# Sample state operations behind the third value tile, masks a head at a time on two engines, and one gate-up weight piece in a place of its own

## Chip, core and metric

The kernel runs on one core of a Trainium2 chip. The metric is device time in microseconds (us) of one execution, as a median over executions. An execution under the hardware profiler gives the trace; its own time is a little longer than the span of the trace, which leaves out what lies before the first and behind the last instruction.

The engines: TensorE (PE in the profile; PEld is its weight load), VectorE (DVE), ScalarE (ACT), GpSimd (POOL) and SyncE (SP), which issues most of the transfers between DRAM and SBUF. Each engine works through its own instructions in order and waits where a result or a buffer isn't ready.

## Reference

One inference step of a one-layer decoder: 8 sample tokens, each with a state of its own, and a prompt of 512 tokens, together 520 columns, with a width of 1024.

```python
z = x @ w_in
qk, mv, mi, mf, mo, aq, ak, av, gm, ga = jnp.split(z, split_points(), axis=-1)
qk, conv_state = causal_dwconv(qk, conv_buf, conv_w, conv_b)
mq, mk = jnp.split(qk, 2, axis=-1)
h, C, n, m = mlstm_chunkwise(mq..., mk..., mv..., mi + b_igate, mf + b_fgate, C0, n0, m0)
...
y_a, k_win, v_win = window_attention(aq..., ak..., av..., k_buf, v_buf, attn_sinks, start)
mixed = jax.nn.sigmoid(gm) * y_m + jax.nn.sigmoid(ga) * y_a
x = layer_norm(ALPHA * x + mixed @ w_out, ln1_g, ln1_b)
g, u = jnp.split(x @ w_gate_up, 2, axis=-1)
ffn = (jax.nn.silu(g) * u) @ w_down
ple = jax.nn.sigmoid(x @ w_ple_gate) * (p @ w_ple)
x = layer_norm(ALPHA * x + ffn + ple, ln2_g, ln2_b)
```

Inside `mlstm_chunkwise` the weights of a chunk are `exp(dmat - m_t)` with a causal mask on `dmat`, and the new state is, per head, `decay_prev * n + sum(w_state * k)` and the same with `k` times `v` for `C`. For a sample token that is one step: `n_new = d * n + w * k`, `C_new = d * C + w * k v`. All is float32.

## The kernel before

**Number format.** A float32 product is made of three products in a faster format: each operand is split into a high part (`split`, line 218, a copy on ScalarE) and the rest (line 219, a subtraction on VectorE or GpSimd), and `mm3`/`mm3ab` (lines 228, 245) add hi·hi, hi·lo and lo·hi. So a weight must be split before TensorE can use it.

**Weights.** They come in blocks of 1 MB through SP's queue into `raw`, a ring of two buffers. `prep_next` splits the next piece of 128 columns into rings `whi` and `wlo` of three buffers each, or into a place of its own where `dest[piece]` names one. `get(piece, ahead)` returns a piece and has later ones prepared.

**Tiles of the input projection.** Tile `t` is 128 columns of `z`: 48 matmuls (8 k-steps, three products, two halves of 264 and 256 columns). Tiles 0 to 7 are q and k of the mLSTM (`ev_qk`), 8 to 15 its values (`ev_mv`, `f` 0 to 7), then the attention's and the gates'. Each tile is evicted behind its matmuls. `ev_mv` copies a value tile from PSUM into `stg`, a ring of two buffers (ACT, L984), transposes it back on TensorE (L987, and L992 for the sample tokens), and copies that to `vaug` (VectorE, L988) and to `tmp` (L996), from where a head's 256 sample values go to a DRAM scratch `vsd` (L998).

**Side work.** `sd.run(t)` issues, behind each tile, steps of lists that were added with a first and a last tile:
- `gate_rows`: the gates' prefix sums and stabilisers; the rows go to a DRAM scratch `bcd` (L912) and come back on all partitions as `wdb` (L913, the sample tokens).
- `conv_out`: the last rows before the convolution, transposed, copied (L973) into a buffer of the ring `stg` and sent out.
- `smlstm_prep`: `n` of the sample tokens is loaded and transposed (L1099), `kws` (L1102, L1103) and `nst` (L1104, L1105) are made from it and `wdb`, `qn` (L1106), and `nst` is transposed back (L1109) and sent out (L1113).
- `ml0`, once a head: two rows of `bcd` on all partitions (L1036, L1037), and the causal mask `cmask` (`amaskA` in the profile) added to the first, chunk by chunk, on GpSimd (L1040).
- `ml1` to `ml3`, once a head and chunk of 128 tokens: the prompt's mLSTM; L1054 is the exponential of a masked chunk.
- `sm0`, `sm1`, `sm2`, once a head and 4 sample tokens: `sm0` loads the state (L1120) and brings `v` from `vsd` to all partitions (L1121, into a `big` buffer); `sm1` scales it by `kws` (ACT, L1141, four times) and updates the state.

Most buffers are rings: `g2` has five of 128x512, `stg` two of 128x520, `tmp` four, PSUM has four banks in `pss` and four in `psm`. A ring's next user waits for the last reader of the buffer, transfers included.

**Order.** In most of the program a scheduler that models the engines' times sets each engine's order from the code and its dependencies; `after(f, ..., f_=[ins])` orders what `f` issues behind `ins` on the engine of `ins`. So a changed step can move others around it. The first gate-up block is a stretch in written order: five weight pieces (`k_gu` to `k_gu + 4`; 3 and 4 in places of their own) are used for the first half of the columns while the first LayerNorm runs, then the second half is computed for four of them. Behind it come pieces from `k_gu + 5` on, each prepared as `get` asks for it, and `tsum`/`tsplit` (L1492, L1496, and L219 on `tf`), which prepare sums of activations for the Strassen products of line 1601.

Of the kernel before, what the change touches and what calls it, by code (L numbers as in the profile page):

```python
# [12 lines left out]
ALU = mybir.AluOpType  # L13
# [4 lines left out]
P = 128  # L18
D = 1024
KD = D // P  # L20
NS = 8
NP = 512
NT = NS + NP
# [6 lines left out]
NCH = NP // P  # L30
# [20 lines left out]
def tile_hybrid_step(  # L51
# [9 lines left out]
    V, S, G, T = nc.vector, nc.scalar, nc.gpsimd, nc.tensor  # L61
# [24 lines left out]
    def ring(tag, n, bufs, p=P):  # L86
        return wp.tile([p, n], F32, tag=tag, name=nm(tag), bufs=bufs)
# [3 lines left out]
    def slab(i):  # L91
        return up.tile([P, U], F32, tag=f"T{i}", name=nm(f"T{i}_"))
# [4 lines left out]
    def v3(t):  # L97
        t3 = t[:, : KD * NT].rearrange("p (j c) -> p j c", j=KD)
        return [t3[:, j, :] for j in range(KD)]
# [89 lines left out]
    def prep_next():  # L189
        i = state["prep"]  # L190
        if i >= len(pieces):
            return
        state["prep"] += 1
        bi_, a, k0, kc, pcol, last = pieces[i]
        if i in dest:
            hi, lo = dest[i]
        else:
            hi = ring("whi", 1024, 3)[:, : kc * pcol].rearrange("p (k n) -> p k n", k=kc)
            lo = ring("wlo", 1024, 3)[:, : kc * pcol].rearrange("p (k n) -> p k n", k=kc)
        split(hi, lo, raws[bi_][:, k0 : k0 + kc, a : a + pcol], G if i in pool_lo else V)  # L200
        ready[i] = (hi, lo)
        if last:
            raws.pop(bi_)
            load_next()

    dest = {}
# [66 lines left out]
    cmask = amaskA[:, :P]  # L273
# [174 lines left out]
    def after(f, *a, f_=None):  # L448
        with ExitStack() as st:
            for ins in f_ or fence:  # L450
                st.enter_context(tc.issue_after(ins))
            f(*a)
# [220 lines left out]
    def g2():  # L673
        return t1([P, 512], "g2", 5)
# [292 lines left out]
    def conv_out():  # L967
        for g in range(2):
            ps = pss()
            for i in range(4):  # L970
                T.transpose(ps[:11, i * P : (i + 1) * P], cvo[:, 4 * g + i, :], ident)
            ost = ring("stg", NT, 2)
            V.tensor_copy(ost[:11, :512], ps[:11, :])  # L973
            nc.sync.dma_start(o_convs[0, :, 2, g * 512 : (g + 1) * 512], ost[:NS, :512])
            nc.sync.dma_start(o_convp[0, 0, :, g * 512 : (g + 1) * 512], ost[NS:11, :512])
            yield
# [4 lines left out]
    def ev_mv(f, pss2):  # L981
        vT = ring("stg", NT, 2)
        for psx, (c0, n) in zip(pss2, HALVES):
            S.activation(vT[:, c0 : c0 + n], psx[:, :n], AF.Copy)  # L984
        ps = pss()
        for c in range(NCH):
            T.transpose(ps[:, c * P : (c + 1) * P], vT[:, NS + c * P : NS + (c + 1) * P], ident)  # L987
        V.tensor_copy(  # L988
            vaug()[:, :, f // 2, (f % 2) * P : (f % 2 + 1) * P], ps.rearrange("p (c d) -> p c d", c=NCH)
        )  # L990
        ps = pss()
        T.transpose(ps[:NS, :P], vT[:, :NS], ident)  # L992
        h = f // 2
        if f % 2 == 0:
            vsx[h] = ring("tmp", 264, 4)
        V.tensor_copy(vsx[h][:NS, (f % 2) * P : (f % 2 + 1) * P], ps[:NS, :P])  # L996
        if f % 2 == 1:
            nc.sync.dma_start(vsd[:, h * DV : (h + 1) * DV], vsx[h][:NS, :DV])  # L998
# [35 lines left out]
    def ml0(h):  # L1034
        bm, it = strip(2 * h), strip(2 * h + 1)
        nc.sync.dma_start(bm, bcd[h, 0].partition_broadcast(P))  # L1036
        nc.sync.dma_start(it, bcd[h, 1].partition_broadcast(P))  # L1037
        for c in range(NCH):
            a0 = NS + c * P
            G.tensor_tensor(bm[:, a0 : a0 + P], bm[:, a0 : a0 + P], cmask, ALU.add)  # L1040
        bmi[h] = (bm, it)

    def ml1(hc):
# [51 lines left out]
    def smlstm_prep():  # L1095
        nr = t1([NS * MH, P], "nr")
        nc.sync.dma_start(nr, st_n[0].rearrange("b h d -> (b h) d"))
        ps = pss()
        T.transpose(ps[:, : NS * MH], nr, ident[: NS * MH, : NS * MH])  # L1099
        nbh = ps[:, : NS * MH].rearrange("p (b h) -> p h b", b=NS)  # L1100
        kS, qS = qkT()[:, 4:8, :NS], qkT()[:, 0:4, :NS]
        V.tensor_tensor(kws, kS, wdb[:, :, 0, :], ALU.mult)  # L1102
        V.tensor_scalar(kws, kws, KSC, None, ALU.mult)  # L1103
        V.tensor_tensor(nst, nbh, wdb[:, :, 1, :], ALU.mult)  # L1104
        V.tensor_tensor(nst, nst, kws, ALU.add)  # L1105
        V.tensor_tensor(qn, nst, qS, ALU.mult)  # L1106
        yield
        ps = pss()
        T.transpose(ps[: NS * MH, :P], nst.rearrange("p h b -> p (h b)"), ident)  # L1109
        ost = ring("tmp", 264, 4)  # L1110
        V.tensor_copy(ost[: NS * MH, :P], ps[: NS * MH, :P])
        for h in range(MH):
            nc.sync.dma_start(o_ns[0, :, h, :], ost[h * NS : (h + 1) * NS, :P])  # L1113
        yield
# [61 lines left out]
            V.scalar_tensor_tensor(y, th[:, :n], 1.0, y, ALU.add, ALU.mult)  # L1176

    mxhi = []
    mxlo = []

    def ev_ga(f, pss2):
        if f == 0:
            mxhi.extend(v3(slab(3)))
        ms = []
        for psx, (c0, n) in zip(pss2, HALVES):
            th = sig_gate(psx, n)
            y = qkT()[:, slot(f), c0 : c0 + n]
            V.scalar_tensor_tensor(th[:, :n], th[:, :n], 1.0, yaT(f)[:, c0 : c0 + n], ALU.add, ALU.mult)
            V.tensor_tensor(y, y, th[:, :n], ALU.add)
        mxlo.append(strip(f))  # L1190
        for c0, n in HALVES:
            y = qkT()[:, slot(f), c0 : c0 + n]
            split(mxhi[f][:, c0 : c0 + n], mxlo[f][:, c0 : c0 + n], y)

    def gen_steps(g):
        return [lambda: next(g, None) for _ in range(16)]
# [21 lines left out]
    sd.add([lambda b=b: after(ple, b) for b in (2, 3)], 3, 4)  # L1218
    sd.add(gen_steps(gate_rows()), 6, 8)
    sd.add(gen_steps(conv_out()), t_mv, t_mv + 2)  # L1220
    sd.add(gen_steps(smlstm_prep()), t_mv, t_mv + 2)
    sd.add([lambda h=h: ml0(h) for h in range(MH)], t_mv + 2, t_mv + 5)
    mlu = [(h, c) for h0 in (0, 2) for c in range(NCH) for h in (h0, h0 + 1)]
    sd.add(skew([ml1, ml2, ml3], mlu), t_mv + 3, t_aq + 2)
# [4 lines left out]
    t = 0  # L1229
    for c0, kind, b in wl:  # L1230
# [29 lines left out]
        if kind == "gm" and b == 3:  # L1260
# [11 lines left out]
            def sub8(t, k):  # L1272
                if len(t) > 1:
                    t, k = t[k // 3], k % 3
                else:
                    t = t[0]
                return t[:, k * 1024 : (k + 1) * 1024].rearrange("p (k n) -> p k n", k=KD)
# [5 lines left out]
    wo = [get(k_wo + k, 0) for k in range(8)]  # L1283
    dest[k_gu + 3] = (sub8(T6, 0), sub8(T6, 1))
    dest[k_gu + 4] = (sub8(T6, 2), sub8(T6, 3))

    rT = [qkT()[:, f, :] for f in range(KD)]
    x1hi, x1lo = xhi, xlo
# [115 lines left out]
    def ev_g(psx, n):  # L1404
        t = ring("gt", 264, 5)
        S.activation(t[:, :n], psx[:, :n], AF.Silu)
        return t
# [13 lines left out]
    with tc.manual_schedule(engines={E.PE, E.DVE, E.Pool, E.Activation}):  # L1421
        n0 = HALVES[0][1]
        pg = [psm() for _ in range(4)]

        def fill(q, k0, k1):
            hi, lo = g0[q]
            for k in range(k0, k1):
                for i, (w, a) in enumerate(((hi, x1hi), (hi, x1lo), (lo, x1hi))):
                    T.matmul(  # L1429
                        pg[q][:, :n0], rr(w[:, k, :]), rr(a[k][:, :n0]),  # L1430
                        start=(k == 0 and i == 0), stop=(k == KD - 1 and i == 2),
                    )

        fill(0, 0, 8)
        fill(1, 0, 2)
        lb.mean(accB)
        fill(1, 2, 8)
        sqs = {}
        for f in range(KD):
            sqs[f] = lb.center(f)  # L1440
            if f > 2:
                lb.accum(f - 1, sqs[f - 1])
        lb.accum(7, sqs[7])
        ts[0, 0] = ev_g(pg[0], n0)
        fill(2, 0, 8)
        lb.var()
        lb.rstd()
        ts[1, 0] = ev_g(pg[1], n0)
        lb.diag()
        fill(3, 0, 6)  # L1450
        lb.bcast()
        fill(3, 6, 8)
        for f in range(KD + 2):
            if f < KD:
                lb.final(f)
            if f >= 2:
                lb.final_lo(f - 2)
        pg.append(psm())
        fill(4, 0, 8)
        for q in (2, 3):  # L1460
            ev_u(q - 2, 0, ts.pop((q - 2, 0)), pg[q])
        ts[4, 0] = ev_g(pg[4], n0)
        c1, n1 = HALVES[1]
        pb4 = [pss(), pss(), psm(), psm()]
        for k in range(KD):
            for q in range(4):
                hi, lo = g0[q]
                for i, (w, a) in enumerate(((hi, x1hi), (hi, x1lo), (lo, x1hi))):
                    T.matmul(
                        pb4[q][:, :n1], rr(w[:, k, :]), rr(a[k][:, c1 : c1 + n1]),  # L1470
                        start=(k == 0 and i == 0), stop=(k == KD - 1 and i == 2),
                    )
# [546 lines left out]
```

## Time and profile before

| | |
|---|---|
| median of three executions | 884.36 us (882.98, 884.54, 884.36) |
| profiled execution, its own time | 885.6 us |
| its span in the trace | 883.5 us |
| mean granted TensorE clock | 0.995 |
| TensorE busy | 866.0 us, 98% of the span, 7082 matmuls |
| VectorE, ScalarE, GpSimd busy | 659.4, 475.5, 156.2 us |
| moved by DMA | 103.69 MB, mean 117 GB/s |

A row of a timeline has the start in us, the busy time of its group, the engine, the line, the operation with output and inputs, their shapes, the count, and in square brackets how long the engine stood idle before it and what ended that. A row of the waits has the waiting group, what released it, then the sum of the waits in us, their count and the longest. The chain of work that ended last is followed back from the last instruction; its shares tell on which engine the end of the kernel hung. The granted clock tells what part of full speed TensorE was given.

### The profile page before, as it was taken

How to read it: one execution, taken by the hardware profiler on the slowest of the kernel's cores; microseconds unless marked ns; L12 is line 12 of the kernel's file. 1: busy time of each engine (PE TensorE's matmuls, PEld its weight loads, DVE VectorE, ACT ScalarE, POOL GpSimd, SP SyncE). 2: the span in 40 equal slices, each digit the busy share in tenths (PEclk: the TensorE clock that was granted, in tenths of full speed). 3: DMA queues.
4: the chain of work that ended last, by engine and by line, in shares of the span. 5: the costliest groups of instructions: out<-in, count | busy, mean ns of one | idle time of the engine just before them, and what ended most of it. 6: DMA issues, size and time to landing. Idle time of an engine off the chain costs nothing.

```text
span 883.5 us, 18583 instructions
## 1 busy us (share of the span) xinstructions
PE 866.0 (98%) x7082; PEld 853.2 (97%) x7082; DVE 659.4 (75%) x1589; ACT 475.5 (54%) x1131; POOL 156.2 (18%) x315
## 2 busy tenths in 40 slices
PE   8999899999999999999999999999999999999996
PEld 7999899999999899999999999999999999999996
DVE  7788555688978676778876968898898875566337
ACT  6545254658777655566525846666666565222120
POOL 5441321115464411221012300000000000000002
PEclk9999999999999999999999999999999999999998
DMA  7642631336465451131520043333334337634212
GB/s 244 223 145 73 194 102 55 55 106 145 157 180 172 145 143 49 49 97 48 191 97 1 23 111 104 112 108 97 107 101 116 108 115 219 202 120 150 96 37 97
DMA packets 125369, 103.69 MB, mean 117 GB/s; under 512 B 7210, under 2 KB 121090, under 8 KB 125256
## 3 DMA queue, kind: packets, MB, share of 16 engines
q1 hardware_dynamic: 125136, 102.38, 38.7%
q8 instruction: 55, 0.90, 0.4%
q14 instruction: 34, 0.28, 0.1%
q10 hardware_dynamic: 144, 0.13, 0.0%
HBM read 91.14 MB, written 12.47 MB: 117 GB/s over the span
## 4 chain that ended last, share of the span: by engine, by line
PE 87%; DVE 5%; DMA 3%; ACT 2%; issue 1%; POOL 1%; SPq 0%; DVEq 0%; ACTq 0%
PE psm L245 41%; PE psm L1601 14%; PE pss L1601 11%; PE psm L228 5%; PE psm L1894 2%; PE psm L1918 2%; PE pss L684 2%; PE pss L737 1%; PE pss L721 1%; PE psm L1429 1%; DMA big<-vsd 1%; PE psm L468 1%; PE pss L1070 1%; PE pss L1074 1%; DMA wdb<-bcd 1%
## 5 line engine op out<-in xcount | busy, mean ns | idle before, releaser
L245 PE MATMUL psm<-T,whi 128*128 128x264 f32 (+1 forms) x1728 | 301.9, 287 | 0.2 <-ACT th L1169 0.2
L245 PEld LDWEIGHTS psm<-T,whi 128*128 128x128 f32 x1728 | 246.8, 189 | 2.1 <-ACT th L1169 0.5
L245 PE MATMUL psm<-T,wlo 128*128 128x256 f32 (+1 forms) x912 | 200.1, 288 | 1.5 <-DVE wlo L219 1.5
L245 PEld LDWEIGHTS psm<-T,wlo 128*128 128x128 f32 x912 | 145.7, 189 | 2.5 <-DVE wlo L219 1.9
L219 DVE TENSOR_TENSOR wlo<-raw,whi 128x1024 fp32r<-128x1024 f32 (+2 forms) x75 | 90.5, 1207 | 66.8 <-ACT whi L218 66.7
L218 ACT ACTIVATE whi<-raw 128x1024 fp32r<-128x1024 f32 (+2 forms) x75 | 77.2, 1034 | 96.9 <-PE psm L245 79.5
L1784 POOL COPY amaskA<-tmp 128x8 f32<-128x8 f32 x8 | 1.5, 189 | 362.9 <-DVE tmp L1782 362.8
L709 POOL TENSOR_SCALAR g<-g,sm 128x256 f32<-128x256 f32 (+1 forms) x64 | 36.2, 579 | 80.2 <-DVE sm L707 23.8
L1585 DVE TENSOR_TENSOR whi<-raw,whi 128x512 fp32r<-128x512 f32 x55 | 37.8, 688 | 11.6 <-ACT whi L1580 10.7
L1580 ACT ACTIVATE whi<-raw 128x512 fp32r<-128x512 f32 x55 | 34.6, 628 | 19.5 <-PE psm L1601 14.4
L1580 ACT ACTIVATE wlo<-raw 128x512 fp32r<-128x512 f32 x55 | 34.6, 629 | 16.3 <-ACT gt L1619 10.2
L1585 DVE TENSOR_TENSOR wlo<-raw,wlo 128x512 fp32r<-128x512 f32 x55 | 37.8, 687 | 6.0 <-ACT wlo L1580 5.6
L702 ACT ACTIVATE g<-g,sm 128x256 f32<-128x256 f32 (+1 forms) x64 | 30.2, 474 | 18.7 <-DVE sm L698 17.7
L245 PE MATMUL psm<-L,whi 128*128 128x264 f32 x192 | 38.7, 282 | 0.0
L219 POOL TENSOR_TENSOR gt<-big,gt 128x256 fp32r<-128x256 f32 x32 | 27.7, 873 | 51.3 <-ACT gt L218 39.5
L1601 PE MATMUL psm<-tf,whi 128*128 128x260 f32 x276 | 36.7, 282 | 0.0
L1601 PE MATMUL psm<-T,wlo 128*128 128x260 f32 x264 | 35.3, 283 | 0.0
L1601 PE MATMUL pss<-tf,whi 128*128 128x260 f32 x264 | 35.3, 283 | 0.0
L1601 PE MATMUL pss<-tf,wlo 128*128 128x260 f32 x264 | 35.3, 283 | 0.0
L1601 PE MATMUL psm<-T,whi 128*128 128x260 f32 x264 | 35.3, 283 | 0.0
L1601 PEld LDWEIGHTS psm<-tf,whi 128*128 128x128 f32 x276 | 34.5, 188 | 0.0
L1601 PE MATMUL psm<-tf,wlo 128*128 128x260 f32 x252 | 33.5, 282 | 0.0
(461 smaller groups left out, 2104.3 us busy)
## 6 DMA issues: line engine op xcount, KB each, us to landing
raw<-in_w_in_dram SPq DMA_DIRECT2D x24, 1024.0 KB
raw<-in_w_gate_up_dram SPq DMA_DIRECT2D x72, 256.0 KB
raw<-in_w_down_dram SPq DMA_DIRECT2D x8, 1024.0 KB
big<-in_state_mlstm_C_dram SPq DMA_DIRECT2D x8, 512.0 KB
big<-vsd SPq DMA_DIRECT2D x8, 512.0 KB
out_dram<-big SPq DMA_DIRECT2D x8, 512.0 KB
raw<-in_w_out_dram SPq DMA_DIRECT2D x4, 1024.0 KB
raw<-in_w_gate_up_dram SPq DMA_DIRECT2D x4, 1024.0 KB
```

Source lines behind the costliest of these rows:

```text
L218: S.activation(rr(hi), src, AF.Copy)
L219: (le or V).tensor_tensor(rr(lo), src, hi, ALU.subtract)
L228: T.matmul(ps[:, :n], rr(w[:, k, wc : wc + P]), rr(a[k0 + k][:, c0 : c0 + n]), start=(i == 0), stop=(i == tot - 1),)
L245: T.matmul(ps[:, :n], rr(w[:, k, wc : wc + P]), rr(a[k0 + k][:, c0 : c0 + n]), start=(i == 0), stop=(i == tot - 1),)
L684: T.matmul(sc[:, a, :w], rr(q[:, a, n * P : (n + 1) * P]), rr(KS[:, kv, hl, (n - 1 + k0) * P : (n + 1) * P]), start=(hl == 0), stop=(hl == 1),
L702: S.activation(pr[:, a, :w], pr[:, a, :w], AF.Exp, bias=sm[:, 2 + a : 3 + a], scale=ASC, accum_out=sm[:, 8 + a : 9 + a],)
L709: G.tensor_scalar(pr[:, a, :w], pr[:, a, :w], sm[:, 12 + a : 13 + a], 0.5, ALU.mult, ALU.mult)
L1580: S.activation(rr(t[:, 0]), wsrcs[i], AF.Copy)
L1585: V.tensor_tensor(rr(lo), wsrcs.pop(i), hi, ALU.subtract)
L1601: T.matmul(ps[:, :TH], rr(w[:, j, :]), rr(x[j]), start=(start and j == 0 and i == 0), stop=(j == 3 and i == 2), skip_group_check=not start,)
L1894: T.matmul(pA[a][:, :264], rr(w[:, a * P : (a + 1) * P]), rr(x[:, :264]), start=(j == 0 and i == 0), stop=(j == KF - 1 and i == 2),)
L1918: T.matmul(pC[c][:, :256], rr(hk[k][x][:, t0 : t0 + P]), rr(w), start=(k == 0 and i == 0), stop=(k == KF - 1 and i == 2),)
```

## The change

Five edits:
1. `conv_out` takes its buffers from `g2` in place of `stg`.
2. `ev_mv` keeps its copy of L988, so that other work can be ordered behind it.
3. `ml0` adds the mask to a head's four chunks in one operation of 128x512 with the mask repeated. Heads 0 and 1 do so on VectorE, behind the latest L988; heads 2 and 3 stay on GpSimd.
4. The steps of `smlstm_prep` are issued at tiles `t_mv + 2` and `t_mv + 3` and ordered behind the copy L988 of the third value tile, where they were issued from `t_mv` on.
5. Piece `k_gu + 5` gets a place of its own (columns of the slabs `mx3[0]`, which held gated activations, and `T5[0]`, which held output projection weights), and it is prepared in the written order of the first gate-up block, behind the fifth gate's eviction.

```diff
@@ conv_out
-            ost = ring("stg", NT, 2)
+            ost = g2()
@@ ev_mv
-        V.tensor_copy(
+        late_t["mv"] = V.tensor_copy(
             vaug()[:, :, f // 2, (f % 2) * P : (f % 2 + 1) * P], ps.rearrange("p (c d) -> p c d", c=NCH)
-        )
+        ).ins
@@ ml0
-        for c in range(NCH):
-            a0 = NS + c * P
-            G.tensor_tensor(bm[:, a0 : a0 + P], bm[:, a0 : a0 + P], cmask, ALU.add)
+        bt = bm[:, NS:].rearrange("p (c t) -> p c t", c=NCH)
+        mb = cmask.unsqueeze(1).to_broadcast([P, NCH, P])
+        if h in (0, 1):
+            after(V.tensor_tensor, bt, bt, mb, ALU.add, f_=[late_t["mv"]])
+        else:
+            G.tensor_tensor(bt, bt, mb, ALU.add)
@@ side work
-    sd.add(gen_steps(smlstm_prep()), t_mv, t_mv + 2)
+    smp = smlstm_prep()
+    sd.add([lambda: after(next, smp, None, f_=[late_t["mv"]]) for _ in range(3)], t_mv + 2, t_mv + 3)
@@ behind the input projection
     dest[k_gu + 4] = (sub8(T6, 2), sub8(T6, 3))
+    dest[k_gu + 5] = tuple(
+        t[:, 6 * NT : 6 * NT + 1024].rearrange("p (k n) -> p k n", k=KD) for t in (mx3[0], T5[0])
+    )
@@ first gate-up block
         ts[4, 0] = ev_g(pg[4], n0)
+        prep_next()
         c1, n1 = HALVES[1]
```

(`mx3` is a new list that keeps the slab `ev_ga` takes.) In the changed kernel the lines from `smlstm_prep` on stand 3 further down, those of the first gate-up block and behind it 9 or 10.

VectorE at the value tiles, before. L988 and L996 are copies of a value tile, L973 the conv rows, L965 the last of a q or k tile, L219 on `wlo` the split of a weight, L1102 to L1106 the sample state's operations, L1111 the copy of the transposed `nst`.

```order
L996 COPY tmp_1298<-pss_1296 8x128
L988 COPY T_195_1231<-pss_1290 128x4x128
L973 COPY stg_1305<-pss_1300 11x512
L973 COPY stg_1314<-pss_1309 11x512
L965 SCALAR_TENSOR_TENSOR T_123_603<-big_1217 128x520
L219 TENSOR_TENSOR wlo_1405<-raw_1165,whi_1404 128x1024
L1102 TENSOR_TENSOR kws_574<-T_123_603,wdb_570 128x32
L1104 TENSOR_TENSOR nst_575<-pss_1320,wdb_570 128x32
L1103 TENSOR_SCALAR kws_574<-kws_574 128x32
L1105 TENSOR_TENSOR nst_575<-nst_575,kws_574 128x32
L1106 TENSOR_TENSOR qn_576<-nst_575,T_123_603 128x32
L1111 COPY tmp_1329<-pss_1327 32x128
```

The same engine after the change, from the split ahead of the second value tile's copies on; L452 is the mask, through a helper.

```order
L219 TENSOR_TENSOR wlo_1388<-raw_1165,whi_1387 128x1024
L996 COPY tmp_1298<-pss_1383 8x128
L988 COPY T_195_1231<-pss_1377 128x4x128
L219 TENSOR_TENSOR wlo_1477<-raw_1165,whi_1476 128x1024
L996 COPY tmp_1452<-pss_1450 8x128
L988 COPY T_195_1231<-pss_1444 128x4x128
L1105 TENSOR_TENSOR kws_574<-T_123_603,wdb_570 128x32
L1107 TENSOR_TENSOR nst_575<-pss_1456,wdb_570 128x32
L452 TENSOR_TENSOR S_228_1471<-S_228_1471,amaskA_101 128x512
L1106 TENSOR_SCALAR kws_574<-kws_574 128x32
L1108 TENSOR_TENSOR nst_575<-nst_575,kws_574 128x32
L1109 TENSOR_TENSOR qn_576<-nst_575,T_123_603 128x32
```

The five sample operations stood behind the first value tile's copies and now stand behind the third's, with one mask among them; the conv rows' copies left `stg`.

ScalarE there, before: L984 is the eviction of a value tile (a pair for each), L218 the high part of a weight, L1054 the exponential of the mLSTM, L1141 the scaling in `sm1`.

```order
L1054 ACTIVATE g_1566<-S_238_1548,colI_566 128x128
L218 ACTIVATE whi_1404<-raw_1165 128x1024
L984 ACTIVATE stg_1391<-psm_1341 128x264
L984 ACTIVATE stg_1391<-psm_1342 128x256
L218 ACTIVATE whi_1479<-raw_1165 128x1024
L984 ACTIVATE stg_1458<-psm_1408 128x264
L984 ACTIVATE stg_1458<-psm_1409 128x256
L218 ACTIVATE whi_1586<-raw_1339 128x1024
L984 ACTIVATE stg_1535<-psm_1485 128x264
L984 ACTIVATE stg_1535<-psm_1486 128x256
L1141 ACTIVATE big_2505<-big_2505,kws_574 128x256 x4
```

And after:

```order
L218 ACTIVATE whi_1387<-raw_1165 128x1024
L984 ACTIVATE stg_1374<-psm_1324 128x264
L984 ACTIVATE stg_1374<-psm_1325 128x256
L218 ACTIVATE whi_1476<-raw_1165 128x1024
L984 ACTIVATE stg_1441<-psm_1391 128x264
L984 ACTIVATE stg_1441<-psm_1392 128x256
L1057 ACTIVATE g_1553<-S_228_1471,colI_566 128x128
L1144 ACTIVATE big_2493<-big_2493,kws_574 128x256 x4
L218 ACTIVATE whi_1580<-raw_1322 128x1024
L984 ACTIVATE stg_1532<-psm_1482 128x264
L984 ACTIVATE stg_1532<-psm_1483 128x256
```

The four scalings (now L1144) moved from behind the fourth value tile's eviction to ahead of it and of the weight's split; of the two exponentials that stood ahead of the second tile's weight (the second of them is the first row of the one list) one stands behind the third tile's eviction.

SyncE's queue there, before: L1037 brings a row of `bcd` to all partitions, L165 loads a weight block, L1152 stores the first sample states.

```order
L1037 DMA S_258_1654<-bcd 128x520
L1037 DMA S_283_1789<-bcd 128x520
L1113 DMA out_dram<-tmp_1329 8x128 x4
L998 DMA vsd<-tmp_1298 8x256
L165 DMA raw_1483<-in_w_in_dram 128x8x256
L1121 DMA big_2505<-vsd 128x4x256
L1152 DMA out_dram<-big_2504 128x4x256
```

And after:

```order
L1037 DMA S_258_1648<-bcd 128x520
L1037 DMA S_283_1780<-bcd 128x520
L998 DMA vsd<-tmp_1298 8x256
L1124 DMA big_2493<-vsd 128x4x256
L165 DMA raw_1480<-in_w_in_dram 128x8x256
L1155 DMA out_dram<-big_2492 128x4x256
L1116 DMA out_dram<-tmp_1465 8x128 x4
```

The four stores of the new `n` went behind the first broadcast of `vsd`, which now also stands ahead of the weight load.

VectorE at the end of the first gate-up block, before: L1496 are sums for the Strassen products, L219 on `tf` their splits, L219 on `wlo` the rest of piece `k_gu + 5`, L1412 the product with the gate in an eviction.

```order
L219 TENSOR_TENSOR L_5597<-tmp_6928,T_899_5657 128x264
L1496 SCALAR_TENSOR_TENSOR T_123_603<-T_123_603 128x260
L219 TENSOR_TENSOR tf_7050<-T_123_603,tf_7048 128x260
L219 TENSOR_TENSOR tf_7049<-T_123_603,tf_7047 128x260
L1496 SCALAR_TENSOR_TENSOR T_123_603<-T_123_603 128x260
L219 TENSOR_TENSOR tf_7049<-T_123_603,tf_7047 128x260
L219 TENSOR_TENSOR wlo_7107<-raw_6702,whi_7106 128x1024
L1412 TENSOR_TENSOR tmp_7039<-gt_7035,psm_6936 128x256
```

And after:

```order
L219 TENSOR_TENSOR L_5585<-tmp_6916,T_899_5645 128x264
L1506 SCALAR_TENSOR_TENSOR T_123_603<-T_123_603 128x260
L219 TENSOR_TENSOR L_5585<-raw_6690,T_899_5645 128x1024
L1506 SCALAR_TENSOR_TENSOR T_123_603<-T_123_603 128x260
L219 TENSOR_TENSOR tf_7045<-T_123_603,tf_7043 128x260
L219 TENSOR_TENSOR tf_7044<-T_123_603,tf_7042 128x260 x2
L219 TENSOR_TENSOR wlo_7102<-raw_6698,whi_7101 128x1024
L1421 TENSOR_TENSOR tmp_7034<-gt_7030,psm_6931 128x256
```

The subtraction of piece `k_gu + 5` (now into a slab, `L`) moved ahead of four of these steps; where it stood there is now the next piece's.

More of the change, by code (lines that the diff above doesn't have):

```diff
@@ L1178, in tile_hybrid_step @@
     mxhi = []
+    mx3 = []
     mxlo = []
@@ L1182, in ev_ga @@
         if f == 0:
-            mxhi.extend(v3(slab(3)))
+            mx3.append(slab(3))
+            mxhi.extend(v3(mx3[0]))
         ms = []
```

## The prediction

> **What bounds the kernel now.** I read the first and fourth parts of the page (busy shares, chain of waits), then all waits of TensorE, then windows and timelines around each.
>
> ```profile
> PE 866.0 (98%) x7082; PEld 853.2 (97%) x7082; DVE 659.4 (75%) x1589; ACT 475.5 (54%) x1131; POOL 156.2 (18%) x315
> PE 87%; DVE 5%; DMA 3%; ACT 2%; issue 1%; POOL 1%; SPq 0%; DVEq 0%; ACTq 0%
> PE pss L1109 <- DVE nst L1105: 2.4, 1, 2.4
> PE psm L245 <- DVE wlo L219: 1.5, 1, 1.5
> PE pss L737 <- ACT T L1027: 1.5, 1, 1.5
> ...
> 91.49 3.91 DMA bcd<-S
> 95.47 6.74 DMA wdb<-bcd
> ```
>
> TensorE is the bound, and the chain is its matmuls from end to end. So other engines' work is free until TensorE stands for it, and a pause taken out reaches the end. Three long pauses lie inside the kernel; the change touches the first two. The last two lines, from the chain, say where the first comes from: the gates go through DRAM and come back as `wdb` only at 95.47 + 6.74 = 102.2.
>
> **First part: the pause at 100.5.** Windows are: length, then busy time of PE, PEld, DVE, ACT, POOL, then granted clock, DMA share, GB/s.
>
> ```profile
> 98.00:100.00 2.00, 2.00 (x19) 2.00 (x19) 0.98 (x1) 0.98 (x2) 0.85 (x3) 1.00 0.65 180
> 100.00:102.00 2.00, 0.64 (x6) 0.43 (x4) 0.24 (x1) 0.00 (x0) 0.00 (x0) 1.00 0.69 261
> 102.00:104.00 2.00, 0.92 (x6) 0.95 (x7) 1.07 (x6) 1.00 (x3) 0.00 (x0) 0.86 0.44 107
> 104.00:106.00 2.00, 2.00 (x11) 1.92 (x10) 1.26 (x2) 1.27 (x3) 1.69 (x3) 0.50 0.76 201
> 106.00:108.00 2.00, 2.00 (x16) 2.00 (x15) 0.87 (x2) 0.00 (x0) 1.01 (x2) 0.79 0.30 48
> ...
> 92.58 0.73 PE L245 MATMUL psm<-T,whi 128*128 128x264 f32 x4
> ...
> 100.24 0.40 PE L245 MATMUL psm<-T,whi 128*128 128x264 f32 x2
> 103.08 0.27 PE L1109 MATMUL pss<-ident,nst 128*32 128x128 f32 x1 [2.45 <-DVE nst L1105]
> ...
> 102.30 0.19 DVE L1102 TENSOR_TENSOR kws<-T,wdb 128x32 f32<-128x32 f32 x1 [2.06 <-DMA wdb<-bcd]
> 102.74 0.19 DVE L1105 TENSOR_TENSOR nst<-nst,kws 128x32 f32<-128x32 f32 x1
> ...
> 102.51 0.66 ACT L984 ACTIVATE stg<-psm 128x264 f32<-128x264 f32 x2 [3.52 <-DVE kws L1102]
> ```
>
> Full-speed matmuls start every 0.12 us, so the next was due at 100.24 + 2 x 0.12 = 100.48; it came at 103.08: 2.6 us. Then the granted clock is low: (1 - 0.86) x 2 + (1 - 0.50) x 2 + (1 - 0.79) x 2 = 1.7 us of array time not granted, 1.55 if the first window counts only for its busy 0.92 us. I take 1.6. The place costs 4.2 us.
>
> The Trainium skill ("TensorE: Matmul & The Clock Gate", Part 1) has the clock fall after an idle window of about 3.4 us; here 2.45 us preceded 0.50. Held strictly to the rule, 1.6 would not belong to this pause and would stay, and the sum would be smaller by that much; that is a rival below. The row decides for me: no other wait stands near it.
>
> Two waits lie on top of each other here. Beside `nst`, the second value tile's eviction (ACT, 102.51) stood 3.52 us: its `stg` buffer was still being sent out by the conv rows, whose transfers were behind the broadcasts in SP's queue. Moving `nst` alone would leave TensorE waiting for this tile's transposes, four matmuls later. The change takes out both (conv rows go to `g2`, whose five buffers nobody needs until the mLSTM units), so I count 4.2 whole.
>
> Does the moved `nst` meet TensorE in time? In the new order I count matmuls from 92.58 at 0.12 us (transposes 0.11): third tile's transposes at 104.7, the `nst` transpose at 109.7, the fourth tile's transposes at 112.9. VectorE copies the third tile until 106.1 (0.68 us), `wdb` is there, and the four small operations (0.19 each at most) with one mask between end by 107.6. Margin 2 us. The mask: 128x512 in SBUF took 688 ns on VectorE (L1585), so two add 1.4 us, beside idle stretches of 2.7 us each. GpSimd loses 8 of 16 mask operations and joins the rest, all off the path. ScalarE's two exponentials no longer stand ahead of the weight split.
>
> ```profile
> L1585 DVE TENSOR_TENSOR whi<-raw,whi 128x512 fp32r<-128x512 f32 x55 | 37.8, 688 | 11.6 <-ACT whi L1580 10.7
> ...
> 113.16 1.23 DVE L219 TENSOR_TENSOR wlo<-raw,whi 128x1024 fp32r<-128x1024 f32 x1 [2.73 <-ACT whi L218]
> ```
>
> **What is late next.** In the new ScalarE order the four L1141 scalings of the first sample unit stand ahead of the split of a weight and the eviction of the fourth tile; before they stood behind. They wait for `big<-vsd`, a broadcast of 512 KB.
>
> ```profile
> 102.22 0.99 SPq L1037 DMA_DIRECT2D S<-bcd  x2
> 103.69 1.48 SPq L1113 DMA_DIRECT2D out_dram<-tmp  x4
> 105.28 0.27 SPq L998 DMA_DIRECT2D vsd<-tmp  x1
> 106.30 0.41 SPq L165 DMA_DIRECT2D raw<-in_w_in_dram  x1
> 107.23 0.39 SPq L1121 DMA_DIRECT2D big<-vsd  x1
> ...
> 113.58 1.71 ACT L1141 ACTIVATE big<-big,kws 128x256 f32<-128x256 f32 x4
> ...
> 196.73 0.62 SPq L1121 DMA_DIRECT2D big<-vsd  x1
> ...
> 208.53 1.71 ACT L1141 ACTIVATE big<-big,kws 128x256 f32<-128x256 f32 x4 [0.77 <-DMA big<-vsd]
> ...
> 288.17 1.79 SPq L1121 DMA_DIRECT2D big<-vsd  x1
> ...
> 296.42 1.71 ACT L1141 ACTIVATE big<-big,kws 128x256 f32<-128x256 f32 x4 [5.37 <-DMA big<-vsd]
> ```
>
> On SP the four L1113 stores move behind `vsd`, the broadcast, a weight load and the L1152 store; nobody reads their target. So `vsd<-tmp` issues at about 103.5, lands two to three us later, and the broadcast issues at about 106. From issue to first use the rows give at most 6.35 us (107.23, behind a 1 MB load), 8.25 and 11.8. Without the megabyte ahead (some 3 us at the 350 GB/s of a full queue, an estimate from the page's peaks) the first becomes about 4: landed at 110. Then 1.6 of scalings, 0.95 of split, 0.35 of eviction: 112.9, when TensorE comes for it. So the cost is nothing up to 4 us after issue and one for one later, plus the 1.6 us of low clock once the pause nears that of the first part. I take 0.4; the range is 0 (at 4) to 1.6 + 7.8 (at 11.8).
>
> **Second part: the pause at 503.** Piece 5 of gate-up.
>
> ```profile
> 503.10 0.40 PE L245 MATMUL psm<-T,whi 128*128 128x264 f32 x2
> 505.02 0.39 PE L245 MATMUL psm<-T,wlo 128*128 128x264 f32 x1 [1.52 <-DVE wlo L219]
> ...
> 502.06 0.42 DVE L1496 SCALAR_TENSOR_TENSOR T<-T 128x260 f32<-128x260 f32 x1
> 502.40 0.76 DVE L219 TENSOR_TENSOR tf<-T,tf 128x260 fp32r<-128x260 f32 x2
> 503.08 0.42 DVE L1496 SCALAR_TENSOR_TENSOR T<-T 128x260 f32<-128x260 f32 x1
> 503.42 0.42 DVE L219 TENSOR_TENSOR tf<-T,tf 128x260 fp32r<-128x260 f32 x1
> 503.76 1.21 DVE L219 TENSOR_TENSOR wlo<-raw,whi 128x1024 fp32r<-128x1024 f32 x1
> ```
>
> The subtraction moves from 503.76 to 502.40, ahead of four 0.34 us steps: 1.36 us earlier. Its first half on ScalarE moves ahead of three `tf` splits, which can delay VectorE by about 0.1. Gain 1.25, and 0.4 us of the pause stays. The four steps pushed back feed the Strassen stage, whose first product is after 522. The own place (feature strips 6 and 7 of two slabs) was last read when the output projection ended near 466, and its next writer is much later: nothing. The evictions at 504.89 and 506.36 fall 1.4 us later, still 1.4 us ahead of the matmuls that need their banks.
>
> **Sum.** 4.2 + 1.25 - 0.4 = 5.05 us off a profiled span of 883.5, whose execution took 885.6. The median of the runs shown is 1.24 us lower; I take the gain off the median: 884.36 - 5.05 = 879.3.
>
> **Rivals.**
> A, slower: the first broadcast takes as long as the one at 196.73. ScalarE then stands to 117.8, TensorE pauses 7.8 us for the fourth tile and pays the low clock, 9.4: 884.36 - 5.45 + 9.4 = 888.3. At 8.25 us (as at 288) it is 884.8, no change. It decides slower from about 9.5 us after issue. For it: the 296 row, where this queue position cost ScalarE 5.37 us and TensorE the third pause. Against: both slow ones had a state load (L1120) issued just ahead; this one was loaded at 82.
> B, half kept: the broadcast comes at 6 us, TensorE pauses 2: 881.
> C, the clock: the 1.6 us low-clock stretch comes from elsewhere and stays: 884.36 - 3.45 = 880.9.
> D, the change doesn't do what it says: VectorE and GpSimd hold each other up in the masks, `nst` is late again.
>
> ```profile
> 93.05 5.80 POOL L1040 TENSOR_TENSOR S<-S,amaskA 128x128 f32<-128x128 f32 x12 [9.83 <-DVE big L962]
> ...
> 104.31 2.70 POOL L1040 TENSOR_TENSOR S<-S,amaskA 128x128 f32<-128x128 f32 x4 [5.46 <-issue]
> 104.95 1.32 DVE L219 TENSOR_TENSOR wlo<-raw,whi 128x1024 fp32r<-128x1024 f32 x1
> ```
>
> Four masks that start beside a two-input subtraction took 2.70 us; twelve earlier took 5.80, so four take 1.9. Two such blocks of 1.9 each behind 107.6 put `nst` at 111.4, a pause of 1.7 and perhaps the low clock: 881 to 882.6. The Trainium skill ("SBUF — State Buffer", Who interferes with whom) has a VectorE operation with two SBUF inputs and a GpSimd one block each other entirely; the 2.70 fits that.
>
> **How the numbers follow.** A change under 0.2% (1.8 us) can't be told from none here. Likeliest, both pauses go and the broadcast costs up to 1.5 us: 0.60, 877.9 to 880.9. C 0.08 and D 0.09 are still faster, B (1.5 to 3.5 us lost) 0.10, mostly faster. Broadcast at 7 to 9.5 us, within 0.2%: 0.07. A: 0.06. So faster 0.82, same 0.11, slower 0.07. The range runs from 877.9 (nothing lost, and run spread) to 882.7, and leaves out A and most of the undecided case.
>
> **What would show it.** Right: no wait of TensorE on `nst`; clock 1.00 from 98 to 110; the second tile's eviction without a wait; a wait on the piece 5 subtraction of about 0.4 us near 498. Wrong: ScalarE's L1141 with a wait on `big<-vsd` ahead of the fourth tile, and TensorE on that tile's `stg`; a low clock with no pause ahead of it; new waits between 115 and 200, where the planner laid out the mLSTM units afresh and I count nothing.

## The result, and the profile after

The changed kernel took 891.2 us (median; 890.2 to 895.38), the kernel before beside it 884.64: a ratio of 1.008, with a 95% interval of 1.0056 to 1.0105. It is slower by some 6.6 us where 5.05 less were forecast. The profiled execution took 890.2 us with a span of 888.4.

The waits of TensorE after the change: waiting group, releaser, then sum, count and longest in us.

```profile
PE pss L1077 <- DVE hs L1010: 3.4, 1, 3.4
PE pss L1151 <- ACT gt L218: 1.7, 1, 1.7
...
PE pss L987 <- ACT stg L984: 1.0, 1, 1.0
...
PE psm L245 <- DVE wlo L219: 0.4, 1, 0.4
```

`nst` is gone from the list, and so is the 1.5 us on `wlo` (piece 5). Three waits are new (the 0.4 on `wlo` is another piece's, at 748), the first two in the prompt's mLSTM and the sample units (L1077 and L1151 stood at L1074 and L1148), where the prediction counted nothing. The windows of the first place are now clean (nothing lost from 98 to 112; two of them first), and the new stretches follow (columns as in the prediction):

```profile
100.00:102.00 2.00, 2.00 (x19) 2.00 (x18) 0.91 (x2) 0.00 (x0) 0.00 (x0) 1.00 0.81 302
104.00:106.00 2.00, 2.00 (x19) 2.00 (x18) 0.48 (x1) 0.00 (x0) 1.30 (x1) 1.00 0.83 224
...
170.00:172.00 2.00, 0.00 (x0) 0.00 (x0) 0.00 (x0) 0.00 (x0) 0.00 (x0) 1.00 0.00 0
174.00:176.00 2.00, 2.00 (x11) 2.00 (x11) 0.89 (x4) 1.42 (x6) 0.98 (x2) 0.50 0.00 0
...
218.00:220.00 2.00, 0.34 (x3) 0.13 (x3) 1.86 (x4) 1.98 (x5) 0.03 (x1) 1.00 0.59 200
222.00:224.00 2.00, 1.74 (x7) 0.77 (x7) 1.85 (x8) 1.98 (x9) 1.97 (x4) 0.50 0.88 189
```

To set executions against each other I cut each span into such windows of 2 us and took what TensorE lost in each: the time it wasn't busy, plus its busy time times (1 - granted clock). Sums by place, in us (e1 to e11 are experiments below):

| place | before | after | e1 | e2 | e5 | e7 | e11 |
|---|---|---|---|---|---|---|---|
| start of the program, 18 to 28 | 1.8 | 3.8 | 3.6 | 3.6 | 1.6 | 3.4 | 3.6 |
| first place, 98 to 108 | 4.0 | 0 | 1.4 | 0 | 0 | 0 | 0 |
| fourth value tile, 112 to 122 | 0 | 1.0 | 0.6 | 1.4 | 1.0 | 3.5 | 0 |
| copy into `Cst`, 168 to 178 | 0 | 5.1 | 0 | 0 | 0 | 0 | 0 |
| second broadcast, 212 to 232 | 0 | 3.6 | 0.3 | 1.6 | 0.4 | 0.3 | 0.4 |
| third pause, 284 to 302 | 1.7 | 0 | 0.9 | 1.8 | 2.3 | 0.9 | 0.1 |
| ahead of the output projection, 422 to 434 | 0 | 0 | 0 | 5.9 | 0 | 0 | 0 |
| piece 5, 502 to 508 | 1.5 | 0 | 0.2 | 0 | 0.2 | 0.2 | 0 |

After less before is +2.0 at the start, -4.0, +1.0, +5.1, +3.6, -1.7 and -1.5: 4.5, where the spans differ by 4.9. The orders at the start are the same in both kernels, so the 2.0 there aren't the change's; the two pauses at 170 and 218, 8.7 us together, are what made it slower.

**The pause at 170.** Timelines of SyncE, VectorE and TensorE in the changed kernel:

```profile
156.68 0.39 SPq L165 DMA_DIRECT2D raw<-in_w_in_dram  x1
158.90 0.37 SPq L1087 DMA_DIRECT2D out_dram<-Cst  x1
159.32 0.73 SPq L1088 DMA_DIRECT2D out_dram<-Cst  x1
...
172.75 0.43 DVE L1079 COPY Cst<-pss 128x257 f32<-128x257 f32 x1 [6.14 <-DMA out_dram<-Cst]
173.23 0.72 PE L1077 MATMUL pss<-T,g 128*128 128x257 f32 x2 [3.43 <-DVE hs L1010]
```

And the chain of waits there (start, length, what took it):

```profile
159.32 13.31 DMA out_dram<-Cst
```

When a head is through, its `C` (L1087) and its `n`, the last column of the same tile `Cst` (L1088), are stored. `n` goes as 128 pieces of 4 bytes. `Cst` is a ring of two, so the fourth head's first copy waits for the second head's stores. These now stand behind a 1 MB weight load, and the store of 512 bytes landed 13.31 us after its issue. VectorE stood 6.14 us at its copy, and TensorE 3.43 behind it.

**The pause at 218.** The timelines of SyncE and ScalarE:

```profile
197.81 0.42 SPq L1088 DMA_DIRECT2D out_dram<-Cst  x1
198.57 0.39 SPq L165 DMA_DIRECT2D raw<-in_w_in_dram  x1
199.06 0.53 SPq L1123 DMA_DIRECT2D big<-in_state_mlstm_C_dram  x1
199.64 0.50 SPq L1124 DMA_DIRECT2D big<-vsd  x1
...
215.59 1.71 ACT L1144 ACTIVATE big<-big,kws 128x256 f32<-128x256 f32 x4 [4.38 <-DMA big<-vsd]
```

Windows there (the last two columns are DMA share and GB/s):

```profile
200.00:202.00 2.00, 2.00 (x19) 2.00 (x18) 1.94 (x12) 0.87 (x3) 0.00 (x0) 1.00 0.99 10
202.00:204.00 2.00, 2.00 (x19) 2.00 (x18) 1.17 (x8) 1.86 (x9) 0.55 (x1) 1.00 0.60 40
204.00:206.00 2.00, 2.00 (x19) 2.00 (x19) 1.16 (x4) 1.80 (x5) 1.79 (x4) 1.00 0.54 26
210.00:212.00 2.00, 2.00 (x20) 1.98 (x19) 0.81 (x2) 0.90 (x3) 1.24 (x3) 1.00 1.09 364
```

Here a head's 4-byte store stands ahead of a weight, a state and a broadcast. Up to 208 the DMA engines are half to fully busy and move 10 to 40 GB/s; then the 2 MB behind come at up to 364. The broadcast landed 15.9 us after its issue, ScalarE stood 4.38 us, and the sample unit's matmuls were late.

Both are changes of order on SyncE's queue. Between the second head's stores and the second broadcast, before:

```text
L1084 DMA out_dram<-Cst_1669 128x256
L1085 DMA out_dram<-Cst_1669 128x1
L165 DMA raw_2242<-in_w_in_dram 128x8x256
L165 DMA raw_2554<-in_w_in_dram 128x8x256
...
L165 DMA raw_2955<-in_w_in_dram 128x8x256
L1084 DMA out_dram<-Cst_2087 128x256
L1085 DMA out_dram<-Cst_2087 128x1
```

and after:

```text
L165 DMA raw_2230<-in_w_in_dram 128x8x256
L1087 DMA out_dram<-Cst_1660 128x256
L1088 DMA out_dram<-Cst_1660 128x1
L165 DMA raw_2542<-in_w_in_dram 128x8x256
...
L1087 DMA out_dram<-Cst_2075 128x256
L1088 DMA out_dram<-Cst_2075 128x1
L165 DMA raw_2943<-in_w_in_dram 128x8x256
```

The first time a weight load went ahead of the stores, the second time the stores went ahead of one. No edit names either; the scheduler laid the mLSTM units out anew.

### The profile page after: what moved, and what is told of

The parts are those of the page before. It is cut to its first block, busy times and chain, and to the rows that moved or that the text cites. A ratio compares the mean times of both kernels' runs of the same rounds, so it can differ in the third digit from the quotient of the medians.

```text
span 888.4 us, 18572 instructions
## 1 busy us (share of the span) xinstructions
PE 870.3 (98%) x7082; PEld 855.9 (96%) x7082; DVE 661.5 (74%) x1591; ACT 476.3 (54%) x1131; POOL 153.0 (17%) x301
## 4 chain that ended last, share of the span: by engine, by line
PE 79%; DMA 8%; DVE 6%; ACT 4%; issue 1%; SPq 1%; POOL 1%; DVEq 0%; ACTq 0%; POOLq 0%
PE psm L245 35%; PE psm L1611 14%; PE pss L1611 10%; PE psm L228 5%; DMA big<-vsd 4%; PE psm L1904 2%; PE psm L1928 2%; DMA out_dram<-Cst 1%; PE pss L737 1%; PE psm L468 1%; PE pss L684 1%; PE pss L721 1%; PE psm L1438 1%; DMA raw<-in_w_down_dram 1%; DMA T<-in_x_prompt_dram 1%
## 5 line engine op out<-in xcount | busy, mean ns | idle before, releaser
L245 PE MATMUL psm<-T,whi 128*128 128x264 f32 (+1 forms) x1696 | 297.0, 287 | 0.2 <-DVE Qbd L671 0.2
L245 PEld LDWEIGHTS psm<-T,whi 128*128 128x128 f32 x1696 | 242.0, 189 | 2.1 <-issue 0.7
L245 PE MATMUL psm<-T,wlo 128*128 128x264 f32 (+1 forms) x896 | 194.3, 288 | 0.4 <-DVE wlo L219 0.4
L245 PEld LDWEIGHTS psm<-T,wlo 128*128 128x128 f32 x896 | 142.9, 190 | 1.2 <-DVE wlo L219 0.7
L219 DVE TENSOR_TENSOR wlo<-raw,whi 128x1024 fp32r<-128x1024 f32 (+1 forms) x74 | 90.0, 1217 | 63.4 <-ACT whi L218 63.0
L218 ACT ACTIVATE whi<-raw 128x1024 fp32r<-128x1024 f32 (+1 forms) x74 | 76.1, 1033 | 94.0 <-PE psm L245 76.5
L219 POOL TENSOR_TENSOR gt<-big,gt 128x256 fp32r<-128x256 f32 x32 | 28.5, 902 | 53.3 <-ACT gt L218 32.1
```

Of the source, the lines that this page charges most:

```text
L218: S.activation(rr(hi), src, AF.Copy)
L219: (le or V).tensor_tensor(rr(lo), src, hi, ALU.subtract)
L245: T.matmul(ps[:, :n], rr(w[:, k, wc : wc + P]), rr(a[k0 + k][:, c0 : c0 + n]), start=(i == 0), stop=(i == tot - 1),)
```

## Experiments

**e1: the change without the mask edit.** The other four edits.

```diff
-        bt = bm[:, NS:].rearrange("p (c t) -> p c t", c=NCH)
...
+            G.tensor_tensor(bm[:, a0 : a0 + P], bm[:, a0 : a0 + P], cmask, ALU.add)
```

> The change without its third edit (masks stay on GpSimd, 128x128 each). Its order on SyncE's queue is that of before at the two places where the changed kernel has it otherwise (weight load against the stores of head 1, stores of head 2 against weight load, state load and broadcast). Theory Q (queue order: the two new pauses, 5.1 and 3.7 us with the low clock behind them, come from where the 4-byte stores of n stand among the loads): both are absent, the first part gives 4.2 less 1.2 for the late broadcast, piece 5 gives 1.3, so 4.3 below before: 880.3, between 879 and 881.5. Rival M (the masks themselves hold VectorE and GpSimd up): also about 880. Rival P (the sample state operations, moved back, push the mLSTM units back): about 890, as the change.

Measured: 883.45, ratio 0.9975 (0.996 to 0.9989). Both new pauses are absent with the old queue order, as theory Q says, and rival P falls. The time is above its range: the gain is 2.2 and not 4.3. A pause at the first place stayed (SyncE, ScalarE, then TensorE), and that place costs less in most executions than the 4.2 that the expectation takes (see the account of the first part).

```profile
98.10 0.30 SPq L974 DMA_DIRECT2D out_dram<-g  x1
...
98.89 0.40 ACT L1054 ACTIVATE g<-S,colI 128x128 f32<-128x128 f32 x1 [4.43 <-DMA out_dram<-g]
...
100.57 0.71 PE L987 MATMUL pss<-ident,stg 128*128 128x128 f32 x4 [1.42 <-ACT stg L984]
```

With the masks where they were, an mLSTM exponential stands ahead of the second tile's eviction. Its row names a store of the conv rows, which would mean that they hold its `g2` buffer, but the first of these stores was issued only 0.8 us before. In e12 the same exponential waits the same 4.43 us and its row names the mask on GpSimd; in before it waited 3.15 us for that mask. So the wait on `stg` became a wait on a mask, and the mask edit is what moves the exponential out of the way.

**e2: n stored once.** The whole change, with

```diff
-            nc.sync.dma_start(o_np[0, 0, h].unsqueeze(1), C[:, DV : DV + 1], allow_slow_non_contiguous=True)
+            V.tensor_copy(nall[:, h : h + 1], C[:, DV : DV + 1])
+            if h == MH - 1:
+                pt = pss()
+                T.transpose(pt[:MH, :P], nall, ident)
...
+                nc.sync.dma_start(o_np[0, 0], nrow[:MH, :P])
```

> The whole change, but the prompt's n of each head is copied to a column of a small tile, and the four are transposed and stored once, in rows of 512 bytes, where each head stored 128 pieces of 4 bytes. Q: no wait of VectorE on the stores of C and n near 170, the broadcast near 200 lands within 10 us, 8.8 us come back: 880 to 882, and below before by 3 to 5. M: the masks are as in the change, so 889 to 891. P: 889 to 891 too.

Measured: 889.93, ratio 1.0051 (1.0038 to 1.0064): a miss for Q by its time. The pauses at 170 and 218 are gone (the nearest is 1.6 us at 230), but the scheduler now put the last attention step behind the last gate matmuls, and TensorE stood ahead of the output projection (its timeline, then a window):

```profile
426.39 0.59 PE L228 MATMUL psm<-T,L 128*128 128x264 f32 x1 [2.51 <-ACT L L218]
```

```profile
428.00:430.00 2.00, 2.00 (x11) 2.00 (x11) 2.00 (x3) 1.49 (x3) 0.00 (x0) 0.50 0.05 16
```

That cost 5.9 with the low clock. An edit that moves the order can't be judged by its time alone, so e5 keeps the order.

**e3: piece 5 alone**, on the kernel before (the fifth edit as in the diff above).

> Before with the fifth edit alone (piece 5 of gate-up in its own place). The trace of the change had 1.34 us less from the first gate-up block to the first Strassen product. If that holds alone, 1.3 below before: 883.3 (882.9 to 883.8). If the sums pushed back cost it again later (0.5 us appeared near 747 in the trace of the change), 883.8 to 884.6.

Measured: 883.12, ratio 0.9983 (0.9969 to 0.9997): -1.5 (0.3 to 2.7), as expected.

**e4: the masks alone**, on the kernel before (the third edit as above, and the second, which it needs).

> Before with the mask edit alone (with the kept copy that it is ordered behind). SyncE's order around the stores of n is that of before. Q: no new pause at 170 or 218, the time within 1 us of before: 884 to 885.5. M: 4 to 9 us slower, 888 to 893.

Measured: 885.08, ratio 0.9997 (0.9987 to 1.0007). The masks cost nothing; rival M falls.

**e5: a row in place of the pieces.** The order of every engine is that of the change. The row is the first of `C`, so this kernel leaves `n` out of its output; so do e6, and e9 and e10 for one head.

```diff
-            nc.sync.dma_start(o_np[0, 0, h].unsqueeze(1), C[:, DV : DV + 1], allow_slow_non_contiguous=True)
+            nc.sync.dma_start(o_np[0, 0, h].unsqueeze(0), C[0:1, :P])
```

> The whole change with every instruction on every engine in the same order; only the four stores of the prompt's n send one row of 512 bytes (the first row of C, so n itself is left out) where they sent 128 pieces of 4 bytes. The second run had both new pauses gone, but its new order put 5.9 us of another pause at 424, behind the last attention step, so it told nothing by its time. Theory Q (the 4-byte stores, by where they stand on SyncE's queue): the wait of VectorE on Cst near 170 and the late broadcast near 215 go, 5.1 and 3.6 us, so 882 to 883.5, below before. Rival R (the new order of the engines itself, whatever the stores): the pauses stay, 889 to 891.

Measured: 882.03, ratio 0.9972 (0.9956 to 0.9987). Same instructions in the same order, the same 512 bytes a head, and 9 us less than the change (timelines of VectorE, SyncE and ScalarE, then two windows):

```profile
166.10 0.41 DVE L1079 COPY Cst<-pss 128x257 f32<-128x257 f32 x1
...
192.15 0.27 SPq L1088 DMA_DIRECT2D out_dram<-Cst  x1
...
193.99 0.49 SPq L1124 DMA_DIRECT2D big<-vsd  x1
...
205.45 1.70 ACT L1144 ACTIVATE big<-big,kws 128x256 f32<-128x256 f32 x4
```

```profile
194.00:196.00 2.00, 2.00 (x20) 2.00 (x19) 1.94 (x12) 0.98 (x3) 0.00 (x0) 1.00 0.99 310
196.00:198.00 2.00, 2.00 (x19) 2.00 (x18) 1.17 (x8) 1.52 (x9) 0.55 (x1) 1.00 1.08 368
```

The copy into `Cst` and the scalings have no wait, the broadcast is there within 11.5 us, and in the two windows from 2 to 6 us behind the store's issue 310 and 368 GB/s are moved, where it was 10 and 40 (200 to 204 in the change). This decides for Q against R.

**e6: the same stand-in store in the kernel before.**

> The kernel before with the same stand-in stores and otherwise the same order on every engine. Q: its two stores that matter stood where nothing waited long, but the third pause (1.5 to 1.7 us near 297, on a broadcast behind a 1 MB load) is not theirs; so 0 to 1 below before: 884.3 to 885.3. If n's stores cost in any order (R2: each holds the queue up by 6 to 8 us, and that is paid in small waits all over): 2 to 4 below, 881 to 883.

Measured: 884.66, ratio 1.0 (0.9982 to 1.0017). In the old order the 4-byte stores cost nothing; R2 falls. It is where they stand, not that they are there.

**e7: the change, n stored late in rows.** As e2, but copied on GpSimd and stored behind tile 28:

```diff
+    sd.add([n_out], 28, 28)
```

> The whole change, n of each head copied aside on GpSimd, transposed and stored once in rows behind tile 28; the last attention step stands 40 matmuls ahead of the output projection, as in before (41). Q: like the fifth run, 881 to 883.5, with no pause at 170 and none at 218. R: 889 to 891.

Measured: 882.79, ratio 0.9985 (0.9973 to 0.9997), within the expected range: with neither of the two pauses.

**e8: piece 5 and n late**, without the other edits.

> Before with the fifth edit and n stored late in the same way, the sample state operations and masks where they were. Q: piece 5 gives 1.3 to 2.2 as in the third run, the rest 0 to 1: 882 to 883.5, no better than the third run's 883.1 by more than 1. R2: 880 to 881.

Measured: 883.26, ratio 0.9983 (0.9968 to 0.9997): e3's time, so late `n` gives nothing by itself.

**e9 and e10: the row for one head only**, in the change's order.

```diff
+            if h == 1:
+                nc.sync.dma_start(o_np[0, 0, h].unsqueeze(0), C[0:1, :P])
+            else:
```

> The whole change in the same order, with the one-row store (n left out) for head 1 alone. Q says that head 1's store, behind a 1 MB weight load, holds the copy into Cst up: the 5.1 us near 170 go, the 3.6 us near 220 stay: about 5 below the change and 2 to 3 above the fifth run, 884.5 to 887. If the two pauses have one cause between them, the time is the fifth run's (882) or the change's (891).

> The same for head 2 alone. Q: head 2's store ahead of a weight, a state and a broadcast delays the broadcast; its 3.6 us go, the 5.1 us near 170 stay: 886 to 888.5. With one cause between them: 882 or 891.

Measured: e9 884.25, ratio 0.9998 (0.9986 to 1.0011); e10 885.78, ratio 1.0013 (0.9999 to 1.0028). Both lie a little under their ranges and between e5 and the change. In e9 the `Cst` copy is free and the broadcast late; in e10 it is the other way round:

```profile
166.55 0.41 DVE L1079 COPY Cst<-pss 128x257 f32<-128x257 f32 x1
...
210.05 1.71 ACT L1147 ACTIVATE big<-big,kws 128x256 f32<-128x256 f32 x4 [4.06 <-DMA big<-vsd]
```

```profile
172.25 0.43 DVE L1079 COPY Cst<-pss 128x257 f32<-128x257 f32 x1 [4.92 <-DMA out_dram<-Cst]
...
210.66 1.70 ACT L1147 ACTIVATE big<-big,kws 128x256 f32<-128x256 f32 x4
```

So there are two causes, one store each. Against e5, e9 is 0.26% longer (2.3 us; it lost 2.3 at 212 to 220) and e10 0.41% (3.6 us; 3.8 at 170 to 178). The two add up to 5.9 us, less than the 9.5 between e5 and the change by their ratios. With one store alone each pause was shorter, and the one in e9 had a clock of 1.00 in all its windows, where the change's had 0.50; why both grow together wasn't settled.

**e11: e7 with the first scalings behind the fourth tile's eviction**, by ordering them behind it on ScalarE.

```diff
+            if hg == (0, 0):
+                after(scaled, f_=[late_t["ev", 3]])
```

> The seventh run (whole change, n stored once behind tile 28) with the first unit's four scalings ordered behind the fourth value tile's eviction on ScalarE, as they stood in before. The pause of 1.0 to 1.8 us at 114 (with 1.7 us of low clock behind it in one of the profiles) goes, nothing else changes: 1 to 2 below the seventh run's 882.8, 880.8 to 882. If that eviction only waits for something else then, no change: 882.8.

Measured: 880.45, ratio 0.9954 (0.9939 to 0.9969), a little under the range. This is the best version: 4.1 us off the kernel before. ScalarE still waits for the broadcast, but behind the eviction, and TensorE doesn't stop:

```profile
112.72 1.71 ACT L1146 ACTIVATE big<-big,kws 128x256 f32<-128x256 f32 x4 [2.49 <-DMA big<-vsd]
```

```profile
114.00:116.00 2.00, 2.00 (x18) 1.94 (x17) 2.00 (x7) 1.35 (x5) 1.18 (x2) 1.00 0.23 65
```

**e12: e11 without the mask edit.**

> The same without the mask edit (masks on GpSimd). The first run had a pause of 1.4 us at 100 there, since an exponential ahead of the second tile's eviction waited for a buffer of g2 that the conv rows now hold. That stays, so 1 to 1.5 above the eleventh run: 882 to 883. If the mask edit has no part in the first pause: the same as the eleventh.

Measured: 882.66, ratio 0.9972 (0.9958 to 0.9986), with e1's 1.42 us lost at 98 to 102, but the row of the exponential names the mask and not a buffer of `g2` as expected:

```profile
99.41 0.40 ACT L1054 ACTIVATE g<-S,colI 128x128 f32<-128x128 f32 x1 [4.43 <-POOL S L1040]
```

The mask edit is worth about 2 us here: 1.4 by the exponential that it takes out of the second tile's way, and the rest, with 1.0 us lost at the third pause, isn't shown to be its.

## Why the prediction was wrong

**The step that failed: "new waits between 115 and 200, where the planner laid out the mLSTM units afresh and I count nothing".** It named the place of the first of the two pauses (the second, at 218, lies beyond its 200) and gave it neither price nor chance. Measured, the pauses at 170 and 218 cost 5.1 and 3.6 us. The prediction followed SyncE's queue as far as L1152; the swaps stand some ten transfers on, in the same listing, and the kernel's own words for the store of `n` (`allow_slow_non_contiguous`) could have told what to look for. That the 4-byte stores are the cause, by where they stand, is shown by e5, e9 and e10 in the change's order and e6 in the old one.

**Rival A had the right kind and the wrong place.** It feared a late broadcast in this queue, at the first one and from the state load. The first landed after 6.0 us, which is rival B's figure, and cost 1.0 and not B's 2 or the 0.4 taken (SyncE, ScalarE and TensorE in the changed kernel):

```profile
106.35 0.37 SPq L1124 DMA_DIRECT2D big<-vsd  x1
...
112.47 1.71 ACT L1144 ACTIVATE big<-big,kws 128x256 f32<-128x256 f32 x4 [3.99 <-DMA big<-vsd]
...
115.45 0.70 PE L987 MATMUL pss<-ident,stg 128*128 128x128 f32 x4 [1.02 <-ACT stg L984]
```

That it cost half of B's figure is luck: TensorE, behind its slower start, was free for the tile at 114.43 where the prediction had it come at 112.9. In e10 the same pause was 2.03 us, in e7 1.83 with 1.7 of low clock. The second broadcast, 15.9 us, had no term.

**First part: the mechanism held, the size was one execution's.** `nst` and the second tile's eviction no longer stop TensorE, and it took the mask edit as well as `g2` (e1, e12). "Whose five buffers nobody needs until the mLSTM units" overlooked that two exponentials of these units stand there, but no run shows a wait that is surely for these buffers; the exponential waited for its mask. But 4.2 came from one profile. In others of programs that leave these steps where they were, the pause was mostly shorter; TensorE's wait for `nst` in e3 and in e4:

```profile
103.09 0.27 PE L1109 MATMUL pss<-ident,nst 128*32 128x128 f32 x1 [1.25 <-DVE nst L1105]
```

```profile
102.06 0.27 PE L1112 MATMUL pss<-ident,nst 128*32 128x128 f32 x1 [1.34 <-DVE nst L1108]
```

By the windows the place lost 4.0 us in before, 1.4 in e3, 1.3 in e4, 1.5 in e6 and 4.5 in e8 (98 to 110): 2.5 in the mean. In e6 TensorE stood 0.30 us for `nst` and 1.16 for the second tile's `stg`, so both waits that the prediction laid on top of each other are there. In e3 the pause ends at 103.09 as in before at 103.08, though TensorE ran 1.2 us later there after a slower start: the gates' way through DRAM set the end, and a late TensorE only waits less. Less the new pause at 114 (0.6 to 3.5, 1.6 in the mean of after, e1, e2, e5, e7, e9 and e10) that leaves about 1, and e5 (-2.5, of which e3's 1.5 are piece 5) agrees.

**Second part: right.** From the last L1469 (499.92) to the first L1601 (522.16) it was 22.24 us, and in the changed kernel (505.73, 526.62) 20.89: 1.35 less, where 1.25 were forecast. The wait fell from 1.52 to 0.16 us, where the prediction wrote 0.4 (its own 1.52 less 1.25 is 0.27):

```profile
509.47 0.39 PE L245 MATMUL psm<-T,L 128*128 128x264 f32 x1 [0.16 <-DVE L L219]
```

e3 has this edit alone and gained 1.5.

**Rivals C and D.** The low clock did go with the pause, so C falls; e3 and e4, with half the pause, had a clock of 1.00 behind it. D falls with e4: masks on VectorE cost nothing measurable. Its row of 2.70 us is 0.8 more than four masks took elsewhere, beside a subtraction of 1.32 us: a slowing, and not a block for the whole of it.

The sum was 5.05 off; e11, with the swaps and the first broadcast's wait taken away, is 4.1 us (2.7 to 5.4) below the before beside it by its ratio. So most of the gain was there, and three side effects of the order ate it. That 4.1 lies near 5.05 is in part luck: the first place is worth 2.5 and not 4.2 in the mean, and in e11's profile the third pause, which the sum doesn't count, is gone too (0.1 where before lost 1.7).

Of 128 pieces of 4 bytes, the Trainium skill ("DMA: Bandwidth & Descriptors", Rules for kernel authors) says that a non-contiguous last dimension becomes one descriptor per element and should be made contiguous; the same page (Queues, rings and completion order) has each DMA engine take descriptors in ring order. The runs agree: 10 to 40 GB/s for 8 us with the next loads behind (after), 368 GB/s with a row in its place (e5).

## What to carry to other kernels

Where a scheduler sets the order, compare the whole order of the transfer queue before and after, not only the part that the edit names, and price every transfer that swapped places with a store of small pieces or a large load. Take a pause's size from more than one execution: where a transfer sets its end, an earlier delay shortens it. To test a cause in such a kernel, make an edit that leaves every engine's order as it is (e5), since one that moves it (e2) brings waits of its own.

## What the runs showed of the hardware

The store of `n` landed 13.3 us after its issue, 6.6 us after the last packet that the windows show (DMA share 0.00 from 166 on); what it waited for then wasn't settled.

The low clock after a pause isn't a matter of the pause's length alone. At the same place 1.83 us without work had it behind (e7, its windows first) and 2.03 us had not (e10):

```profile
114.00:116.00 2.00, 0.42 (x3) 0.36 (x4) 1.77 (x5) 2.00 (x6) 0.00 (x0) 1.00 0.21 67
118.00:120.00 2.00, 2.00 (x11) 2.00 (x10) 1.82 (x5) 1.34 (x4) 0.72 (x2) 0.50 0.02 4
```

```profile
114.00:116.00 2.00, 0.14 (x2) 0.00 (x0) 1.77 (x6) 2.00 (x5) 0.00 (x0) 1.00 0.35 113
118.00:120.00 2.00, 2.00 (x19) 2.00 (x18) 1.92 (x5) 1.83 (x4) 1.33 (x2) 1.00 0.05 13
```

The Trainium skill ("TensorE: Matmul & The Clock Gate", Part 1) has the clock fall after an idle window of about 3.4 us, and says that the window runs freely and that its effect varies between runs. No run here shows the window itself; the traces show the fall after 1.83 and 2.45 us and none after 2.03.
